# A batch of eight two-layer experts: smaller pieces for the last two w2, and x cast and transposed inside a first layer

## The chip, the cores and the metric

The kernel runs on one core of one Trainium2 chip. The metric is the device time of one execution in microseconds. A profile is one further execution, of which the hardware profiler recorded every instruction and every DMA packet.

In the profile the engines are PE (TensorE, matmuls), PEld (its weight loads, which overlap the matmuls), DVE (VectorE), ACT (ScalarE), POOL (GpSimd) and SP (SyncE). L83 is line 83 of the kernel before.

## The reference

```python
n_experts, capacity, hidden, expert_hidden = 8, 256, 512, 2048
x:  (8, 256, 512)    w1: (8, 512, 2048)    w2: (8, 2048, 512)    all float32

h = np.matmul(x, w1)
h = np.maximum(h, 0)
return np.matmul(h, w2).astype(np.float32)
```

For each of eight experts, 256 rows of 512 go through a first layer to 2048 values with a ReLU, and through a second layer back to 512. Each w1 and each w2 is 4 MB of float32, so 67 MB of weights are read once and used once.

## The kernel before, in words

Weights are cast from float32 to bfloat16 by the DMA that loads them, on POOL's queue (`load_w1`, L57, and `load_w2`, L63). x is loaded as float32 on SP's queue (`load_x`, L53) and cast to bfloat16 by ACT (L67). Results are written as float32 on SP's queue (L121), the last half of the last one on ACT's (L119).

**One expert.** `transpose_x(e)` casts x (L67), transposes it in eight 128x128 blocks on TensorE through an identity (L71) into one PSUM tile `pt_tr`, and copies that to SBUF as `xt_sb` on DVE (L75). `first_layer(e)` makes the hidden values transposed, in eight groups `g` of two blocks of 128 hidden values. Each group is eight matmuls (L83: two blocks, four steps over the 512 inputs) into a PSUM tile `pt_h`, and one ReLU into `ht_sb`: on ACT for even groups (L93), on DVE for odd ones (L91). `second_layer(e)` runs 16 steps `kt` over the hidden values (called row groups of w2 here), each with two matmuls (L107), one for each half `mt` of the 256 rows, into the PSUM tiles `po[0]` and `po[1]`. DVE copies the first to `out_sb` (L115), ACT the second (L116).

**How rows are dealt.** Weights and x are viewed so that each partition holds consecutive rows of its matrix in memory: partition p of w2 has rows 16p to 16p+15. A slice `lo:hi` of row groups is therefore one contiguous run for each partition.

**The order of the work.** The kernel's engines run in the order in which the code issues: it is a manual schedule, and the framework adds only the semaphore waits. The order of the layers is

```python
    for e in range(E - 3):
        order += [(1, e), (2, e)]
    order += [(1, e) for e in range(E - 3, E)] + [(2, e) for e in range(E - 3, E)]
```

so experts 0 to 4 run layer by layer, and then come the first layers of experts 5, 6 and 7 and after them their second layers. All weight loads are issued ahead in the same order, each held back only by its buffer: there are four buffers for w1 and four for w2. At most eight loads are in flight on POOL's queue; each later one waits until the one eight issues before it has landed. The x of four experts is loaded at the start, and that of expert e + 4 after the second layer of expert e.

Before the change `transpose_x(e + 1)` is called after `first_layer(e)`. On ACT the cast stands behind the ReLUs of that first layer; on TensorE the transposes stand between the first layer and what follows, and wait for the cast.

The w2 of the last expert comes in four pieces of 6, 5, 3 and 2 row groups; every other weight comes in one DMA. In the last second layer the last four matmuls are put in order of `mt`, so that `po[0]` is finished two matmuls ahead of `po[1]`. Its output is written in two halves.

**Buffers that matter.** PSUM: four tiles `ps_h` (for `pt_h`) and four `ps_o` (for `pt_tr` and `po` in turn). SBUF: two each of `x_bf` and `xt_sb`, four of `ht_sb`, three of `out_sb`, four of `x_sb`.

Of the kernel before, what the change touches and what calls it, by code (L numbers as in the profile page):

```python
# [1 line left out]

# [5 lines left out]


@with_exitstack  # L10
def kernel(
    ctx: ExitStack,
    tc: tile.TileContext,
    x: bass.AP,
    w1: bass.AP,
    w2: bass.AP,
    out: bass.AP,
):
    nc = tc.nc
    P = 128  # L20
    bf = mybir.dt.bfloat16
    f32 = mybir.dt.float32

    E, C, H = x.shape
    F = w1.shape[2]
    MT = C // P
    KT1 = H // P
    KT2 = F // P
    AHEAD = 4


    x_r = x.rearrange("e (p mt) k -> e p mt k", p=P)
    w1_r = w1.rearrange("e (p kt) n -> e p kt n", p=P)
    w2_r = w2.rearrange("e (p kt) n -> e p kt n", p=P)
    out_r = out.rearrange("e (p mt) n -> e p mt n", p=P)

    const = ctx.enter_context(tc.tile_pool(name="const", bufs=1))
    wpool = ctx.enter_context(tc.tile_pool(name="weights", bufs=4))
    xpool = ctx.enter_context(tc.tile_pool(name="xs", bufs=AHEAD))
    tpool = ctx.enter_context(tc.tile_pool(name="xts", bufs=2))  # L40
    hpool = ctx.enter_context(tc.tile_pool(name="hidden", bufs=4))
    opool = ctx.enter_context(tc.tile_pool(name="outs", bufs=3))
    ps_h = ctx.enter_context(tc.tile_pool(name="ps_h", bufs=4, space=bass.MemoryType.PSUM))
    ps_o = ctx.enter_context(tc.tile_pool(name="ps_o", bufs=4, space=bass.MemoryType.PSUM))

    x_sb, w1_sb, w2_sb, xt, ht = {}, {}, {}, {}, {}


    ctx.enter_context(tc.manual_schedule())

    def load_x(e):
        x_sb[e] = xpool.tile([P, MT, H], f32, tag="x", name="x_sb")
        nc.sync.dma_start(x_sb[e][:], x_r[e])  # L53

    def load_w1(e):
        w1_sb[e] = wpool.tile([P, KT1, F], bf, tag="w1", name="w1_sb")
        nc.gpsimd.dma_start(w1_sb[e][:], w1_r[e])  # L57

    def load_w2(e):
        w2_sb[e] = wpool.tile([P, KT2, H], bf, tag="w2", name="w2_sb")  # L60
        cuts = (0, KT2) if e < E - 1 else (0, 6, 11, 14, 16)
        for lo, hi in zip(cuts, cuts[1:]):
            nc.gpsimd.dma_start(w2_sb[e][:, lo:hi, :], w2_r[e, :, lo:hi, :])  # L63

    def transpose_x(e):
        x_bf = tpool.tile([P, MT, H], bf, tag="xb", name="x_bf")
        nc.scalar.copy(x_bf[:], x_sb[e][:])  # L67
        pt = ps_o.tile([P, KT1, MT, P], bf, tag="ps_o", name="pt_tr")
        for kt in range(KT1):
            for mt in range(MT):  # L70
                nc.tensor.transpose(  # L71
                    pt[:, kt, mt, :], x_bf[:, mt, kt::KT1], identity[:]
                )
        xt[e] = tpool.tile([P, KT1, C], bf, tag="xt", name="xt_sb")
        nc.vector.tensor_copy(xt[e][:], pt[:].rearrange("p k m q -> p k (m q)"))  # L75

    def first_layer(e):
        ht[e] = hpool.tile([P, KT2, C], bf, tag="ht", name="ht_sb")
        for g in range(KT2 // 2):
            ph = ps_h.tile([P, 2, C], f32, tag="ps_h", name="pt_h")  # L80
            for i in range(2):
                for kt in range(KT1):
                    nc.tensor.matmul(  # L83
                        ph[:, i, :],
                        w1_sb[e][:, kt, 2 * g + i::KT2],
                        xt[e][:, kt, :],
                        start=(kt == 0),
                        stop=(kt == KT1 - 1),
                    )
            if g % 2:  # L90
                nc.vector.tensor_relu(ht[e][:, 2 * g:2 * g + 2, :], ph[:])  # L91
            else:
                nc.scalar.activation(  # L93
                    ht[e][:, 2 * g:2 * g + 2, :], ph[:],
                    mybir.ActivationFunctionType.Relu,
                )

    def second_layer(e):
        last = e == E - 1
        po = [  # L100
            ps_o.tile([P, H], f32, tag="ps_o", name=f"pt_o{mt}") for mt in range(MT)
        ]
        order = [(kt, mt) for kt in range(KT2) for mt in range(MT)]
        if last:
            order = order[:-4] + [(kt, mt) for mt in range(MT) for kt in (KT2 - 2, KT2 - 1)]
        for kt, mt in order:
            nc.tensor.matmul(  # L107
                po[mt][:],
                ht[e][:, kt, mt * P:(mt + 1) * P],
                w2_sb[e][:, kt, :],  # L110
                start=(kt == 0),
                stop=(kt == KT2 - 1),
            )
        o = opool.tile([P, MT, H], f32, tag="o", name="out_sb")
        nc.vector.tensor_copy(o[:, 0, :], po[0][:])  # L115
        nc.scalar.copy(o[:, 1, :], po[1][:])  # L116
        if last:
            nc.sync.dma_start(out_r[e, :, 0, :], o[:, 0, :])
            nc.scalar.dma_start(out_r[e, :, 1, :], o[:, 1, :])  # L119
        else:  # L120
            nc.sync.dma_start(out_r[e], o[:])  # L121


    order = []
# [4 lines that stand above are left out]
    for e in range(AHEAD):  # L129
        load_x(e)  # L130
    for layer, e in order:
        (load_w1 if layer == 1 else load_w2)(e)
        if (layer, e) == (1, 0):
            identity = const.tile([P, P], bf, name="identity")
            make_identity(nc, identity)
    transpose_x(0)
    for layer, e in order:
        if layer == 1:
            first_layer(e)
            if e + 1 < E:  # L140
                transpose_x(e + 1)
        else:
            second_layer(e)
            if e + AHEAD < E:
                load_x(e + AHEAD)


# [1 line left out]
_INS = ['x', 'w1', 'w2']  # L149
_OUTS = [((8, 256, 512), 'float32')]  # L150


# [23 lines left out]
```

## Time and profile before

| | |
|---|---|
| device time, median of 9 runs | 188.21 us (186.73 to 188.51) |
| the profiled execution: its own time | 188.45 us |
| the profiled execution: span from first to last instruction | 186.7 us (186.67) |
| TensorE matmuls, busy | 131.1 us, 70% of the span |
| ACT, DVE, POOL busy | 32.7, 33.2 and 10.9 us |
| mean granted TensorE clock | 0.936 |
| moved by DMA | 42.06 MB (bytes written), 225 GB/s in the mean |
| weights on POOL's queue | 33.56 MB, 84.6% of 16 engines' span |
| x and outputs on SP's queue | 8.13 MB, 11.6% |
| waits of first layers for w1 (L83) | 29.9 us in 8 waits |
| waits of second layers for w2 (L107) | 10.1 us in 6 waits |
| waits of transposes for the cast (L71) | 10.6 us in 8 waits |
| cast of one x on ACT | 1038 ns |

The span leaves out 1.78 us of the execution's own time. In the page each digit of a row is the busy share of one fortieth of the span, in tenths. Lines of an order of time give the start and the length in microseconds, then engine, line, operation, output and input, and in brackets the idle time of the engine before it and what ended it. Lines that run on without idle time are put together, with a count.

### The profile page before, as it was taken

Reading aid. Unit: us, or ns where it says so; the run is one execution under the profiler, and the core shown is the slowest. Engines: PE = TensorE matmul, PEld = TensorE weight load, DVE = VectorE, ACT = ScalarE, POOL = GpSimd, SP = SyncE. Lnnn points to the kernel's source line nnn. Section 1 sums busy time; section 2 is a strip of 40 time slices with the busy share of each in tenths; the row PEclk is TensorE's granted clock in tenths of the full one; section 3 lists DMA queues with packets and bytes.
Section 4 is the critical chain, followed back from the end, with each engine's and each line's share of the span. In section 5 each row is a group of like instructions: output and inputs, shape, how many; then the busy total and the mean of one; then the engine's idle time right before and its main releaser. Section 6 shows DMA issues by size and latency. Waiting matters only on the chain.

```text
span 186.7 us, 1887 instructions
## 1 busy us (share of the span) xinstructions
PE 131.1 (70%) x825; PEld 90.2 (48%) x832; DVE 33.2 (18%) x48; ACT 32.7 (17%) x49; POOL 10.9 (6%) x25
## 2 busy tenths in 40 slices
PE   0203969488494988749895696929879693959990
PEld 0103954187141884337741594408778691414440
DVE  0100240114101141101411032011433331010101
ACT  3100330124001150102401123012514230010101
POOL 7300010101000000000111101001000000000000
PEclk9999999999879699965999789996999999988999
DMA  6999999999999999999999999999999999999913
GB/s 218 269 215 239 249 215 225 225 236 240 213 274 216 251 231 224 255 219 257 240 218 266 209 262 234 222 266 209 252 231 225 221 225 207 193 215 263 214 58 114
DMA packets 5193, 42.06 MB, mean 225 GB/s; under 512 B 577, under 2 KB 577, under 8 KB 3265
## 3 DMA queue, kind: packets, MB, share of 16 engines
q0 software_dynamic: 2736, 33.56, 84.6%
q1 hardware_dynamic: 2304, 8.13, 11.6%
q10 hardware_dynamic: 144, 0.26, 0.4%
q8 instruction: 6, 0.10, 0.2%
q14 instruction: 3, 0.02, 0.0%
HBM read 71.30 MB, written 4.19 MB: 404 GB/s over the span
## 4 chain that ended last, share of the span: by engine, by line
PE 54%; DMA 25%; another core or an unknown queue 12%; ACT 3%; issue 2%; POOL 1%; DVE 0%; ACTq 0%; POOLq 0%
PE pt_o L107 28%; PE pt_h L83 25%; DMA w_sb<-in_w_dram 25%; ACT x_bf L67 3%; PE pt_tr L71 2%; POOL w_sb L57 1%; DVE out_sb L115 0%; POOL w_sb L63 0%; POOL identity masks.py:199 0%; POOL identity masks.py:197 0%; ACT ht_sb L93 0%; ACTq L116 0%; POOLq masks.py:199 0%; ACTq L93 0%
## 5 line engine op out<-in xcount | busy, mean ns | idle before, releaser
L83 PE MATMUL pt_h<-xt_sb,w_sb 128*128 128x256 bf16 x512 | 66.4, 297 | 29.9 <-DMA w_sb<-in_w_dram 29.9
L83 PEld LDWEIGHTS <-w_sb 128*128 128x128 bf16 x512 | 60.5, 148 | 36.9 <-DMA w_sb<-in_w_dram 33.0
L107 PE MATMUL pt_o<-w_sb,ht_sb 128*128 128x512 bf16 x249 | 59.4, 395 | 10.5 <-DMA w_sb<-in_w_dram 10.1
L107 PEld LDWEIGHTS <-ht_sb 128*128 128x128 bf16 x256 | 25.8, 101 | 42.3 <-issue 15.6
L91 DVE TENSOR_SCALAR ht_sb<-pt_h 128x512 bf16<-128x512 f32 x32 | 22.1, 692 | 75.1 <-PE pt_h L83 75.1
L93 ACT ACTIVATE ht_sb<-pt_h 128x512 bf16<-128x512 f32 x32 | 19.1, 597 | 74.6 <-PE pt_h L83 74.6
L116 ACT COPY out_sb<-pt_o 128x512 f32<-128x512 f32 x8 | 4.7, 586 | 72.5 <-PE pt_o L107 72.5
L115 DVE COPY out_sb<-pt_o 128x512 f32<-128x512 f32 x8 | 5.5, 692 | 63.2 <-PE pt_o L107 63.2
L71 PE MATMUL pt_tr<-identity,x_bf 128*128 128x128 bf16 x64 | 5.5, 233 | 10.6 <-ACT x_bf L67 10.6
L71 PEld LDWEIGHTS <-x_bf 128*128 128x128 bf16 x64 | 4.1, 119 | 12.2 <-ACT x_bf L67 12.2
L57 POOL DMA_DIRECT2D w_sb<-in_w_dram x8 | 4.4, 556 | 75.9 <-PE pt_h L83 75.1
L67 ACT CAST x_bf<-x_sb 128x1024 bf16<-128x1024 f32 x8 | 8.3, 1038 | 2.2 <-DMA x_sb<-in_x_dram 2.2
L63 POOL DMA_DIRECT2D w_sb<-in_w_dram x11 | 6.0, 543 | 39.8 <-DMA w_sb<-in_w_dram 24.1
L75 DVE COPY xt_sb<-pt_tr 128x1024 bf16<-128x1024 bf16 x8 | 5.5, 692 | 11.3 <-PE pt_tr L71 11.3
L67 ACT ACT_TABLE_LOAD x1 | 1.3, 1283 | 0.7 <-PEq L160 0.7
masks.py:199 POOL TENSOR_SCALAR_AFFINE_SELECT identity<-identity 128x128 bf16<-128x128 bf16 x1 | 0.3, 288 | 0.1
masks.py:197 POOL MEMSET identity<- 128x128 bf16 x1 | 0.2, 223 | 0.0
L160 POOL MEMSET const-float32-0.0<- 128x1 f32 x1 | 0.1, 100 | 0.2 <-issue 0.2
L160 POOL MEMSET const-uint8-127<- 128x1 uint8 x1 | 0.1, 103 | 0.0
L160 POOL MEMSET const-bfloat16-1.0<- 128x1 bf16 x1 | 0.1, 102 | 0.0
L160 POOL MEMSET const-float32-1.0<- 128x1 f32 x1 | 0.1, 100 | 0.0
## 6 DMA issues: line engine op xcount, KB each, us to landing
w_sb<-in_w_dram POOLq DMA_DIRECT2D x15, 2048.0 KB, 66.6
x_sb<-in_x_dram SPq DMA_DIRECT2D x8, 512.0 KB, 25.6
out_dram<-out_sb SPq DMA_DIRECT2D x7, 512.0 KB, 15.0
w_sb<-in_w_dram POOLq DMA_DIRECT2D x1, 768.0 KB, 70.0
w_sb<-in_w_dram POOLq DMA_DIRECT2D x1, 640.0 KB, 70.0
w_sb<-in_w_dram POOLq DMA_DIRECT2D x1, 384.0 KB, 60.6
w_sb<-in_w_dram POOLq DMA_DIRECT2D x1, 256.0 KB, 51.1
out_dram<-out_sb ACTq DMA_DIRECT2D x1, 256.0 KB, 2.6
```

What stands on the lines that cost most here:

```text
L57: nc.gpsimd.dma_start(w1_sb[e][:], w1_r[e])
L63: nc.gpsimd.dma_start(w2_sb[e][:, lo:hi, :], w2_r[e, :, lo:hi, :])
L67: nc.scalar.copy(x_bf[:], x_sb[e][:])
L71: nc.tensor.transpose(pt[:, kt, mt, :], x_bf[:, mt, kt::KT1], identity[:])
L75: nc.vector.tensor_copy(xt[e][:], pt[:].rearrange("p k m q -> p k (m q)"))
L83: nc.tensor.matmul(ph[:, i, :], w1_sb[e][:, kt, 2 * g + i::KT2], xt[e][:, kt, :], start=(kt == 0), stop=(kt == KT1 - 1),)
L91: nc.vector.tensor_relu(ht[e][:, 2 * g:2 * g + 2, :], ph[:])
L93: nc.scalar.activation(ht[e][:, 2 * g:2 * g + 2, :], ph[:], mybir.ActivationFunctionType.Relu,)
L107: nc.tensor.matmul(po[mt][:], ht[e][:, kt, mt * P:(mt + 1) * P], w2_sb[e][:, kt, :], start=(kt == 0), stop=(kt == KT2 - 1),)
L115: nc.vector.tensor_copy(o[:, 0, :], po[0][:])
L116: nc.scalar.copy(o[:, 1, :], po[1][:])
L160: nc = _bacc.Bacc("TRN2", target_bir_lowering=False, num_devices=1)
```

## The change

It has three parts.

1. w2 of expert 6 comes in three DMAs (6, 5 and 5 row groups) instead of one, and w2 of expert 7 in seven (4, 4, 3, 2, 1, 1 and 1) instead of four.
2. The last second layer runs its matmuls in the same plain order as the others.
3. The cast and the transposes part company. `first_layer(e)` starts with the cast of x of the next expert, and halfway, before its fifth group, it issues the transposes of that x and the copy to `xt_sb`. Nothing is transposed after a first layer any more.

```diff
     def load_w2(e):
         w2_sb[e] = wpool.tile([P, KT2, H], bf, tag="w2", name="w2_sb")
-        cuts = (0, KT2) if e < E - 1 else (0, 6, 11, 14, 16)
+        cuts = {E - 2: (0, 6, 11, 16), E - 1: (0, 4, 8, 11, 13, 14, 15, 16)}.get(e, (0, KT2))
         for lo, hi in zip(cuts, cuts[1:]):
             nc.gpsimd.dma_start(w2_sb[e][:, lo:hi, :], w2_r[e, :, lo:hi, :])
 
+    def cast_x(e):
+        xb[e] = tpool.tile([P, MT, H], bf, tag="xb", name="x_bf")
+        nc.scalar.copy(xb[e][:], x_sb[e][:])
+
     def transpose_x(e):
-        x_bf = tpool.tile([P, MT, H], bf, tag="xb", name="x_bf")
-        nc.scalar.copy(x_bf[:], x_sb[e][:])
         pt = ps_o.tile([P, KT1, MT, P], bf, tag="ps_o", name="pt_tr")
         for kt in range(KT1):
             for mt in range(MT):
                 nc.tensor.transpose(
-                    pt[:, kt, mt, :], x_bf[:, mt, kt::KT1], identity[:]
+                    pt[:, kt, mt, :], xb[e][:, mt, kt::KT1], identity[:]
                 )
...
     def first_layer(e):
+        if e + 1 < E:
+            cast_x(e + 1)
         ht[e] = hpool.tile([P, KT2, C], bf, tag="ht", name="ht_sb")
         for g in range(KT2 // 2):
+            if g == KT2 // 4 and e + 1 < E:
+                transpose_x(e + 1)
             ph = ps_h.tile([P, 2, C], f32, tag="ps_h", name="pt_h")
...
         order = [(kt, mt) for kt in range(KT2) for mt in range(MT)]
-        if last:
-            order = order[:-4] + [(kt, mt) for mt in range(MT) for kt in (KT2 - 2, KT2 - 1)]
         for kt, mt in order:
...
+    cast_x(0)
     transpose_x(0)
     for layer, e in order:
         if layer == 1:
             first_layer(e)
-            if e + 1 < E:
-                transpose_x(e + 1)
         else:
             second_layer(e)
```

More of the change, by code (lines that the diff above doesn't have):

```diff
@@ L44 @@
     ps_o = ctx.enter_context(tc.tile_pool(name="ps_o", bufs=4, space=bass.MemoryType.PSUM))
-    x_sb, w1_sb, w2_sb, xt, ht = {}, {}, {}, {}, {}
+    x_sb, xb, xt, w1_sb, w2_sb, ht = {}, {}, {}, {}, {}, {}
     ctx.enter_context(tc.manual_schedule())
```

## The prediction

> **What bounds the kernel now.** I read the page first (slices and queues), then the order of time of TensorE, then a table of stretches at the end, then the issues of the weights. Part 2 and 3 of the page:
>
> ```profile
> PEclk9999999999879699965999789996999999988999
> DMA  6999999999999999999999999999999999999913
> ...
> q0 software_dynamic: 2736, 33.56, 84.6%
> ```
>
> The DMA engines are full in every slice but the first and the last two, and POOL's queue, which carries only weights, has 84.6% of all 16 engines' time. TensorE is idle 30% of the span. So up to about 177 us the kernel runs at the pace of the weight stream, and what TensorE saves there it waits for in the next layer. The end is different. TensorE's order of time, and the last copies:
>
> ```profile
> 135.38 0.64 PE L71 MATMUL pt_tr<-identity,x_bf 128*128 128x128 bf16 x8 [0.75 <-ACT x_bf L67]
> 137.19 7.21 PE L83 MATMUL pt_h<-xt_sb,w_sb 128*128 128x256 bf16 x64 [1.18 <-DMA w_sb<-in_w_dram]
> 145.15 0.64 PE L71 MATMUL pt_tr<-identity,x_bf 128*128 128x128 bf16 x8 [0.75 <-ACT x_bf L67]
> 146.99 7.21 PE L83 MATMUL pt_h<-xt_sb,w_sb 128*128 128x256 bf16 x64 [1.20 <-DMA w_sb<-in_w_dram]
> 157.08 7.07 PE L107 MATMUL pt_o<-w_sb,ht_sb 128*128 128x512 bf16 x31 [2.88 <-DMA w_sb<-in_w_dram]
> 166.40 15.65 PE L107 MATMUL pt_o<-w_sb,ht_sb 128*128 128x512 bf16 x63 [2.26 <-DMA w_sb<-in_w_dram]
> ...
> 175.02 0.69 DVE L115 COPY out_sb<-pt_o 128x512 f32<-128x512 f32 x1 [10.37 <-PE pt_o L107]
> 175.18 0.59 ACT L116 COPY out_sb<-pt_o 128x512 f32<-128x512 f32 x1 [10.42 <-PE pt_o L107]
> 182.13 0.59 ACT L116 COPY out_sb<-pt_o 128x512 f32<-128x512 f32 x1 [6.37 <-PE pt_o L107]
> 182.14 0.69 DVE L115 COPY out_sb<-pt_o 128x512 f32<-128x512 f32 x1 [6.42 <-PE pt_o L107]
> ```
>
> The reader should see that every layer before 166 starts on a DMA wait, and that from 166.40 the second layers of experts 6 and 7 run as one block of 63 recorded matmuls without a wait. Stretches of that end (us, busy time and count of PE, PEld, DVE, ACT, POOL, then clock, DMA share, GB/s):
>
> ```profile
> 157.03:164.14 7.11, 7.01 (x31) 3.13 (x32) 0.17 (x1) 0.00 (x0) 0.00 (x0) 1.00 1.04 221
> 164.14:166.40 2.26, 0.00 (x1) 0.00 (x0) 0.52 (x1) 0.59 (x1) 0.00 (x0) 1.00 0.87 179
> 166.40:175.20 8.80, 8.74 (x32) 3.60 (x33) 0.18 (x1) 0.02 (x1) 0.00 (x0) 0.81 1.04 238
> 175.20:177.50 2.30, 2.30 (x12) 1.08 (x11) 0.52 (x1) 0.57 (x1) 0.00 (x0) 1.00 0.88 241
> 177.50:182.10 4.60, 4.55 (x22) 1.86 (x19) 0.00 (x0) 0.00 (x0) 0.00 (x0) 1.00 0.11 44
> ```
>
> TensorE idles 2.26 us for the whole of w2 of expert 6, then runs at a mean clock of 0.81 (0.50 for about 3.4 us), and from 177.5 on the DMA engines have almost nothing left while TensorE still has 4.6 us to do. The weights are all there at 177.5, as the issues tell:
>
> ```profile
> 126.37 0.53 POOL L63 DMA_DIRECT2D w_sb<-in_w_dram  x1 [10.20 <-DMA w_sb<-in_w_dram]
> ```
>
> ```profile
> w_sb<-in_w_dram POOLq DMA_DIRECT2D x1, 256.0 KB, 51.1
> ```
>
> 126.37 + 51.1 = 177.5: the last piece (two row groups) waits 4 us for TensorE. So the bound changes hands at 166: weights before, TensorE after, with 2.26 us lost to idling and about 1.7 us to the half clock (3.4 us at half speed).
>
> **What the Trainium skill says.** "TensorE: Matmul & The Clock Gate", Part 1 (the HAM clock gate): a free-running window of about 3.4 us halves the clock after too idle a window. The trace agrees in size (0.50 for 3.4 us from 166.3), and shows it for a window that was about 37% busy; one 46% busy before 156 stayed at full clock. "DMA: Bandwidth & Descriptors", Queues, rings and completion order: each engine takes turns between queues, packet by packet. The trace agrees: the output of expert 5, issued at 164.8 behind the weights, takes until 173.2 to land, that of expert 6, issued when the weights are nearly through, 3.0 us. The same page, Anatomy of one DMA: about 2.0 us fixed per DMA from GpSimd, mostly the write receipt. Here it does not add up along the queue: the three-row piece issued at 115.65 lands 60.6 later at 176.3, the two-row piece at 177.5, 1.2 us apart.
>
> **The change, part by part.**
>
> *w2 of expert 6 in three pieces (6, 5, 5 row groups).* w2 of 5 lands at 157.03, of 6 at 166.36: 0.583 us a row group, so the pieces land near 160.5, 163.5 and 166.4. Its second layer can follow that of expert 5 at 164.14 at once. Two pieces are there, the third is needed 22 matmuls of 0.213 us later, at 168.8. At 32 x 0.213 = 6.8 us it ends at 171.0 rather than 175.0. The idling and the half clock both go; what is late next is w2 of expert 7.
>
> *w2 of expert 7 in seven pieces (4, 4, 3, 2, 1, 1, 1).* Total bytes are the same. I count time per DMA engine (eight packets each per piece) from the packet records: packets of 16,384, 6,144, 5,120, 3,072 and 2,048 bytes written take 1.227, 0.474, 0.398, 0.248 and 0.173 us; consecutive starts are some 0.02 closer (0.154 at 2,048), so time is nearly in proportion to bytes. A one-row packet of 1,024 bytes is not shown. Bounds: half of the 2,048 one, 0.086, and all of it, 0.173. I take the lower end, since the final output's 2,048-byte packets need only 0.086 and proportion holds down to 2,048. With semaphore packets (0.02 each) five more pieces then cost some 0.2 us; at the upper end 24 x 0.087 = 2.1 us.
>
> *The output of expert 6 moves.* With TensorE done at 171.0 it is issued at 171.8 instead of 175.8. Then its eight packets per engine of 0.165 us, 1.3 us, go in between those of w2 of 7. Before, its first packet went at 176.63, when the slowest engine was 0.5 us from its end. So w2 of 7 is delayed by about 1.1 us (bounds 0 and 1.3). Last piece: 177.5 + 1.1 + 0.2 = 178.8.
>
> *Last matmuls.* TensorE starts expert 7 at 171.0. The first four row groups landed near 169.3, eight near 172.5, eleven near 174.5, then 176.4, 177.3, 178.1, 178.8; a row group costs it 0.43. It keeps up and waits for each late piece. End: 178.8 + 0.05 + 2 x 0.213 = 179.3 instead of 182.07: 2.8 us.
>
> *The plain order of the last two row groups* puts the end of po0 one matmul before po1, not two. Before, the two-matmul lead gave nothing: both copies started at 182.13. In expert 5 with the plain order the copies start 0.2 apart (163.97, 164.18), so this may give 0.1. The output then follows as before: 182.14 to 186.67 is 4.5 us.
>
> *Cast and transposition inside the first layer.* Eight casts of 1.04 us (ACT), 64 transposes (0.64 us per expert on TensorE) and eight copies of 0.69 us (DVE) stay, moved. TensorE no longer waits 0.75 us seven times plus a few tenths for the last relu. Some 1.6 us leave the gap between layers, 0.64 of it entering the first layer. What hides this is the wait for weights that follows (1.18, 1.20, 2.88 us above; 3.7 before experts 4 and 5): I price it at nothing; without that cover it would be worth 7 x 1.0 = 7 us or so. ACT's cast now stands ahead of the four relus, which free pt_h for TensorE. It waits for x, last for expert 7: issued at 101.4, at most 27.4 later (128.8), needed before the relu at 138.3. Expert 1 needs it by 18.8 and x of it is among the first loads. DVE has the copy between relus; with 0.69 in each 1.75 us it has room. The release of w1 to POOL comes up to 0.64 later; weights lie 66.6 us (median) in the queue, so none runs dry. SP's outputs and x loads move up to 1.6 us earlier, same bytes.
>
> *POOL's issues.* Five more of 0.53 us. Each waits for the piece eight issues before it; the last for the second piece of expert 6, about 163.5, some 15 us before it is due. Nothing else of use is queued behind.
>
> *Sum.* 186.7 - 2.8 - 0.1 = 183.8 of span. The profiled execution's own time is 188.45 with a span of 186.67, 1.78 outside. 183.8 + 1.78 = **185.6**. The nine times lie in two groups, near 186.8 and near 188.4, 1.7 apart, the cost of one half-clock window; the median of 188.21 stands in the upper group with the profiled one, 0.24 below it. The changed end is set by the stream and shouldn't split so.
>
> **The rivals.**
> - *Half clock in the last layer.* TensorE now waits for pieces, so a window could fall below the busy share. For it: the 37% case. Against: from 174.5 on it has 2.6 us of work in each 3.4 at first, then 2.1 in 3.5, above 46%. Price from 0.43 (the last pair alone) to 1.7: 186.0 to 187.3, say 186.5.
> - *A floor under small packets.* Upper bound above, 2.1 us: 187.7, no change. Against: proportion in five sizes.
> - *The pieces change nothing at TensorE*, if the second layer of 6 still waits for its whole tile: 188.4, or 186.8 in the other group. Against: each group of matmuls in the new program waits on its own piece's semaphore.
> - *Slower: completions in series.* If each one-row piece takes the skill's 2.0 us after the one ahead, instead of 0.7, the last three add 3.9: landing at 182.7, 189.5. It decides in POOL's queue, from a last landing of 181.6 on (no gain), and 182.5 for slower by 0.5%. Against: 1.2 us between the last two pieces above; for: no one-row piece is shown.
>
> **How the numbers follow.** Forecast 0.66 (own range 184.9 to 186.6), half clock 0.14, floor 0.07, nothing changed 0.06, completions 0.07. Half a per cent, 0.94 us, is about what a measurement here can tell: faster is below 187.27, slower above 189.15. Faster: 0.66 + 0.12 + 0.02 + 0.02 = 0.82; slower 0.06 of the completions; the rest, 0.12, the same. From 184.7 to 187.7 leaves out the completions, the unchanged case, the upper part of the floor and 0.03 below.
>
> **What would show it.** Second layer of 6 starting near 164.2 with no wait and full clock; expert 7's starting near 171 and then waiting on DMA, the longest wait about a microsecond; the last piece landing near 178.8; last copies near 179.4; output of 6 issued near 171.8; DMA share full to 178. Wrong if the one-row pieces land over 1 us apart, if a clock of 0.5 appears after 171, or if waits before 157 grow.

## The result, and the profile after

The changed kernel takes 185.8 us (median of 18 runs, 185.6 to 186.23). The kernel before took 186.9 us in the runs beside it (median of 55, 186.66 to 189.0). The ratio is 0.992 (95% interval 0.990 to 0.994). It compares all executions: those of the kernel before lie in two groups, 37 near 186.8 and 18 near 188.4, and the second group draws the ratio below that of the two medians, 0.994. One execution of the kernel before, of 270 us, is left out of everything below. The profiled execution has a span of 183.9 us instead of 186.7, and its own time is 185.71 instead of 188.45; the one before was of the slower group.

The page's slices and POOL's queue, after:

```profile
PEclk9999999969999998897999669997899969999999
DMA  5999999989999999999999999999999998999973
...
q0 software_dynamic: 3456, 33.56, 86.4%
```

In the DMA row the second slice from the end holds 7 tenths instead of 1: the stream and the work now end almost together. The clock's dips now all lie before 151 us; the one near the end is gone.

The order of time of TensorE, and the last copies:

```profile
146.91 8.82 PE L89 MATMUL pt_h<-xt_sb,w_sb 128*128 128x256 bf16 x64 [2.26 <-DMA w_sb<-in_w_dram]
156.59 15.70 PE L111 MATMUL pt_o<-w_sb,ht_sb 128*128 128x512 bf16 x70 [0.86 <-DMA w_sb<-in_w_dram]
172.60 3.30 PE L111 MATMUL pt_o<-w_sb,ht_sb 128*128 128x512 bf16 x14 [0.31 <-DMA w_sb<-in_w_dram]
176.58 2.98 PE L111 MATMUL pt_o<-w_sb,ht_sb 128*128 128x512 bf16 x10 [0.68 <-DMA w_sb<-in_w_dram]
...
170.44 0.69 DVE L119 COPY out_sb<-pt_o 128x512 f32<-128x512 f32 x1 [6.27 <-PE pt_o L111]
170.60 0.59 ACT L120 COPY out_sb<-pt_o 128x512 f32<-128x512 f32 x1 [6.32 <-PE pt_o L111]
179.64 0.59 ACT L120 COPY out_sb<-pt_o 128x512 f32<-128x512 f32 x1 [8.46 <-PE pt_o L111]
179.85 0.69 DVE L119 COPY out_sb<-pt_o 128x512 f32<-128x512 f32 x1 [8.72 <-PE pt_o L111]
```

From 156.59 the second layers of 5 and 6 and the start of 7 run as one block; the wait of 2.26 us ahead of expert 6 is gone. The copies of expert 6 start at 170.4 instead of 175.0. TensorE's waits now lie inside expert 7, and are short. Stretches of the end (us, busy time and count of PE, PEld, DVE, ACT, POOL, then clock, DMA share, GB/s):

```profile
163.65:170.60 6.95, 6.90 (x33) 3.14 (x32) 0.68 (x2) 0.59 (x1) 0.43 (x1) 1.00 1.04 239
170.60:172.60 2.00, 1.69 (x8) 0.69 (x7) 0.53 (x1) 0.59 (x1) 0.00 (x0) 1.00 1.08 236
172.60:177.50 4.90, 4.22 (x18) 1.74 (x18) 0.00 (x0) 0.00 (x0) 0.00 (x0) 1.00 1.09 251
177.50:179.60 2.10, 1.88 (x7) 0.48 (x5) 0.00 (x0) 0.00 (x0) 0.00 (x0) 1.00 0.22 35
```

The clock is whole throughout, and the DMA engines are full until about 177.5, 2 us before TensorE is done. In those 2 us they move little: some of the 16 engines are still at the last pieces while the others have finished. The chain that ended last, in order of time (start, length, what), closes like this:

```profile
163.56 15.37 DMA w_sb<-in_w_dram
178.93 0.04 issue
178.97 0.61 PE pt_o L111 x2
179.58 0.27 issue
179.85 0.69 DVE out_sb L119
```

The last piece lands at 178.93 and two matmuls follow. (Landing times here and below are those of the last of a transfer's 16 semaphore increments in the trace.) Before, TensorE had 4.6 us of work left when the last piece landed (177.47 to 182.07).

### The profile page after: what moved, and what is told of

It is laid out like the page before. It is cut to its first block, busy times and chain, and to the rows that moved or that the text cites. A ratio compares the mean times of both kernels' runs of the same rounds, so it can differ in the third digit from the quotient of the medians.

```text
span 183.9 us, 1894 instructions
## 1 busy us (share of the span) xinstructions
PE 131.2 (71%) x825; PEld 90.9 (49%) x832; DVE 32.5 (18%) x48; ACT 32.8 (18%) x49; POOL 13.5 (7%) x30
## 4 chain that ended last, share of the span: by engine, by line
another core or an unknown queue 38%; DMA 33%; PE 18%; POOL 4%; issue 3%; DVE 0%; POOLq 0%
DMA w_sb<-in_w_dram 33%; PE pt_o L111 9%; PE pt_h L89 9%; POOL w_sb L63 3%; POOL w_sb L57 1%; PE pt_tr L73 0%; DVE out_sb L119 0%; POOL identity masks.py:199 0%; POOL identity masks.py:197 0%; POOLq masks.py:199 0%; POOLq L174 0%; POOLq L63 0%; POOLq L163 0%
## 5 line engine op out<-in xcount | busy, mean ns | idle before, releaser
L89 PE MATMUL pt_h<-xt_sb,w_sb 128*128 128x256 bf16 x512 | 69.7, 303 | 31.2 <-DMA w_sb<-in_w_dram 31.2
L89 PEld LDWEIGHTS <-w_sb 128*128 128x128 bf16 x512 | 61.7, 149 | 39.3 <-DMA w_sb<-in_w_dram 34.4
L111 PE MATMUL pt_o<-w_sb,ht_sb 128*128 128x512 bf16 x249 | 58.4, 387 | 11.9 <-DMA w_sb<-in_w_dram 11.4
L63 POOL DMA_DIRECT2D w_sb<-in_w_dram x16 | 8.6, 540 | 74.0 <-DMA w_sb<-in_w_dram 66.1
L57 POOL DMA_DIRECT2D w_sb<-in_w_dram x8 | 4.4, 556 | 76.2 <-PE pt_h L89 75.4
L73 PEld LDWEIGHTS <-x_bf 128*128 128x128 bf16 x64 | 4.7, 116 | 5.2 <-ACT x_bf L67 5.2
```

What stands on the lines that cost most here:

```text
L73: nc.tensor.transpose(pt[:, kt, mt, :], xb[e][:, mt, kt::KT1], identity[:])
L89: nc.tensor.matmul(ph[:, i, :], w1_sb[e][:, kt, 2 * g + i::KT2], xt[e][:, kt, :], start=(kt == 0), stop=(kt == KT1 - 1),)
L111: nc.tensor.matmul(po[mt][:], ht[e][:, kt, mt * P:(mt + 1) * P], w2_sb[e][:, kt, :], start=(kt == 0), stop=(kt == KT2 - 1),)
```

## The experiments

Each is told as a change of the kernel before or of the changed kernel. Ratios are to the kernel before in the runs beside it, over all executions as above.

**The pieces alone** (of the kernel before):

```diff
-        cuts = (0, KT2) if e < E - 1 else (0, 6, 11, 14, 16)
+        cuts = {E - 2: (0, 6, 11, 16), E - 1: (0, 4, 8, 11, 13, 14, 15, 16)}.get(e, (0, KT2))
```

> The pieces alone: both new lists of cuts, with cast, transposes and the order of the last matmuls as before. Theory (the whole gain comes from the pieces, the moves are hidden by the wait for weights): as the changed kernel, 185.8 us, ratio about 0.993, span near 184, last piece landing near 178.9. Rival (the moves carry a part): at most half of the gain is left, 186.4 or more against 186.9 of the kernel before.

Measured: 186.24 us, ratio 0.994 (0.992 to 0.996), span 184.2, last landing 178.76. That lies between the theory and the rival: the early start of expert 6 and the late last landing are there, but 0.4 us against the changed kernel is missing. Something else in the change carries that, the moves or the plain order.

**The moves alone**: the changed kernel with the old cuts and the old order of the last four matmuls.

```diff
-        cuts = {E - 2: (0, 6, 11, 16), E - 1: (0, 4, 8, 11, 13, 14, 15, 16)}.get(e, (0, KT2))
+        cuts = (0, KT2) if e < E - 1 else (0, 6, 11, 14, 16)
...
         order = [(kt, mt) for kt in range(KT2) for mt in range(MT)]
+        if last:
+            order = order[:-4] + [(kt, mt) for mt in range(MT) for kt in (KT2 - 2, KT2 - 1)]
```

> The moves alone: cast and transposes inside the first layer, old cuts and old order of the last matmuls. Theory: no change, ratio 1.00 within 0.004, since each first and second layer still starts when its weights land (w2 of 5 at 156.5 to 157, w2 of 6 at 166.4). Rival: 0.5 us or more faster.

Measured: 186.81 us, ratio 0.997 (0.994 to 1.000). TensorE's order of time at the end:

```profile
157.77 7.99 PE L113 MATMUL pt_o<-w_sb,ht_sb 128*128 128x512 bf16 x30 [0.22 <-issue]
166.45 13.97 PE L113 MATMUL pt_o<-w_sb,ht_sb 128*128 128x512 bf16 x63 [0.68 <-DMA w_sb<-in_w_dram]
```

Expert 6 starts at 166.45, as before: the moves don't shift the end. The faster groups agree too (medians 186.80 and 186.77); that only 3 of 20 executions lie above 187.7 here, and 28 of 71 of the kernel before, may be chance. This profile also shows the last block of 63 matmuls at full clock (the half-clock window fell into expert 5, 157.1 to 160.5): 13.97 us instead of 15.65 in the profile of the kernel before. Its time, 186.87, is that of the lower group of the kernel before.

**w2 of 6 in pieces, w2 of 7 as before** (of the changed kernel):

```diff
-        cuts = {E - 2: (0, 6, 11, 16), E - 1: (0, 4, 8, 11, 13, 14, 15, 16)}.get(e, (0, KT2))
+        cuts = {E - 2: (0, 6, 11, 16), E - 1: (0, 6, 11, 14, 16)}.get(e, (0, KT2))
```

> The changed kernel, but w2 of expert 7 in its four old pieces (6, 5, 3, 2). Theory: the second layer of 6 still follows that of 5 at once, the end is set by a last piece of two row groups, with four matmuls after it instead of two: 0.4 us later than the changed kernel, 186.2 us, span near 184.3, last landing near 178.7. Rival (the pieces of one row group carry the gain): 186.7 or more.

Measured: 186.12 us, ratio 0.993 (0.991 to 0.995). Without the seven pieces of expert 7, 0.8 of the 1.1 us are still there; the seven add 0.3 us. (This run has the plain order too, so the 0.8 us isn't the worth of expert 6's pieces alone.) The profile fell on an execution of 187.26 us with the clock halved from 156.4 to 163.2:

```profile
158.07 23.00 PE L111 MATMUL pt_o<-w_sb,ht_sb 128*128 128x512 bf16 x93 [0.22 <-issue]
```

TensorE then doesn't wait again and sets the end itself, at 181.1, though the last piece landed at 177.59 (not at the expected 178.7, since the output of 6 was issued later too, at 174.8, and hardly delayed it): an execution with two half-clock windows in expert 5 is bound by TensorE even with the early start.

**w2 of 7 in pieces, w2 of 6 whole** (of the changed kernel):

```diff
-        cuts = {E - 2: (0, 6, 11, 16), E - 1: (0, 4, 8, 11, 13, 14, 15, 16)}.get(e, (0, KT2))
+        cuts = {E - 1: (0, 4, 8, 11, 13, 14, 15, 16)}.get(e, (0, KT2))
```

> The changed kernel, but w2 of expert 6 in one piece. Theory: its second layer starts at 166.4 as before and TensorE sets the end, so the seven pieces of 7 gain nothing: span 186.7 with a half-clock window in the second layer of 6, 185.0 without, ratio about 1.00. Rival (the pieces of 7 carry the gain): span near 184, ratio 0.993.

Measured: 186.61 us, ratio 0.998 (0.995 to 1.001). In the order of time:

```profile
156.51 7.07 PE L111 MATMUL pt_o<-w_sb,ht_sb 128*128 128x512 bf16 x31 [0.81 <-DMA w_sb<-in_w_dram]
166.26 15.66 PE L111 MATMUL pt_o<-w_sb,ht_sb 128*128 128x512 bf16 x63 [2.68 <-DMA w_sb<-in_w_dram]
```

A wait like that of the kernel before (2.68 us, there 2.26) and the same block of 63. The last piece lands at 177.51, as before, and TensorE is done at 181.9. So the small last pieces gain nothing while expert 6 starts late; they need its early start. Against the changed kernel 0.8 us is lost. The faster group has a median of 186.5, 0.26 below that of the kernel before: no matmul waits for a late piece here, so the gain lies elsewhere. The next run traces it to the plain order.

**The old order of the last four matmuls** (in the changed kernel), to find what the pieces alone lacked:

```diff
         order = [(kt, mt) for kt in range(KT2) for mt in range(MT)]
+        if last:
+            order = order[:-4] + [(kt, mt) for mt in range(MT) for kt in (KT2 - 2, KT2 - 1)]
```

> The changed kernel, with only the old order of the last four matmuls put back. With a last piece of one row group the old order leaves three matmuls after its landing, the plain order two. Theory A (this is most of what the pieces alone lacked): one matmul of 0.21 us and little more, 186.0 to 186.25 us. Theory B (the moves of cast and transposes make the difference): as the changed kernel, 185.8 us.

Measured: 186.28 us, ratio 0.994 (0.991 to 0.996). That is the time of the pieces alone (186.24), so the moves add nothing and the plain order is worth 0.45 to 0.5 us. The end of its order of time, where the last piece landed at 179.01:

```profile
179.06 0.81 PE L113 MATMUL pt_o<-w_sb,ht_sb 128*128 128x512 bf16 x3 [0.27 <-DMA w_sb<-in_w_dram]
...
179.94 0.59 ACT L122 COPY out_sb<-pt_o 128x512 f32<-128x512 f32 x1 [8.67 <-PE pt_o L113]
179.95 0.69 DVE L121 COPY out_sb<-pt_o 128x512 f32<-128x512 f32 x1 [8.73 <-PE pt_o L113]
```

Three matmuls follow the landing instead of two: the old order keeps the matmul (14, second half) back behind (15, first half), which needs the last piece. The last matmul ends 0.85 after the landing instead of 0.63, so that is 0.2 us.

The rest comes after the last matmul. From its end to the end of the span it takes 4.64 us here and 4.34 in the changed kernel. With the old order both copies start together and the two halves of the output are issued 0.11 us apart; with the plain order DVE's copy starts 0.21 behind ACT's, and the halves are issued 0.31 apart. (Why DVE's copy starts later there is open.) ACT's half then lands 2.78 after the last matmul instead of 3.33, SyncE's half at much the same distance as before (3.45, 3.50). At the end SyncE waits for one transfer's semaphore after another, for ACT's half first, then for six others, and last for its own half. Its long waits there (us in total, times, longest), with the plain order and with the old one:

```profile
SPq L174 <- DMA out_dram<-out_sb: 1.6, 2, 1.4
SPq L176 <- DMA out_dram<-out_sb: 2.1, 1, 2.1
```

With the plain order it goes through the six others, some 0.06 us each, between the two landings and is free 0.05 us after the last. With the old order the halves land 0.17 apart, and it goes through them after both: it is free 0.31 us after the last. The other profiles agree: from the last matmul to the end of the span the kernel before and the pieces alone take 4.61 and 4.60 us, the runs with expert 6 whole and with the old pieces of 7, which have the plain order, 4.38 and 4.40.

**The output of 6 behind the weights** (in the changed kernel):

```diff
+        elif e == E - 2:
+            nc.gpsimd.dma_start(out_r[e], o[:])
         else:
             nc.sync.dma_start(out_r[e], o[:])
```

> The changed kernel, but the output of expert 6 is issued on POOL's queue, so that its packets stand behind all of w2 of 7 and don't take turns with them. Theory (the early output delays w2 of 7 by 1.1 us): the last piece lands near 177.8 instead of 178.9, and the output of 6 fills the DMA engines between then and 180; span near 182.8, 184.7 us. Rival (the delay comes from the number of small pieces, or from the engines' own spread): last landing unchanged, 178.5 or later, time 185.6 or more. If GpSimd's output DMA is slow to land, it could end last instead, above 184 in span.

Measured: 184.58 us, ratio 0.988 (0.986 to 0.989). In the profile the last piece of w2 of 7 lands at 177.68 instead of 178.93, and the output of 6 at 178.96. The early output's turns cost the weights 1.25 us, and the time falls by 1.2. The profile itself caught an execution of 185.77, with the clock halved from 156.9 to 160.3:

```profile
157.94 21.61 PE L111 MATMUL pt_o<-w_sb,ht_sb 128*128 128x512 bf16 x93 [0.22 <-issue]
```

**The output of 5 as well:**

```diff
-        elif e == E - 2:
+        elif e >= E - 3:
             nc.gpsimd.dma_start(out_r[e], o[:])
```

> As the one before, and the output of expert 5 on POOL's queue too. Theory: another 1.3 us of packets leaves the stream, the last piece would land near 176.5; TensorE, which starts expert 7 near 170.5 with 6.8 us of work, now nearly sets the end (177.4): span 182.2 to 182.6, since 2.6 us of outputs then also meet the last output. Rival: no better than with the output of 6 alone.

Measured: 184.48 us (183.81 to 185.93), ratio 0.989 (0.985 to 0.993). No better in the median, as the rival had it. The reason is TensorE:

```profile
157.48 20.88 PE L111 MATMUL pt_o<-w_sb,ht_sb 128*128 128x512 bf16 x94 [0.81 <-DMA w_sb<-in_w_dram]
```

The last piece lands at 177.19, but TensorE works from 157.48 to the end without a wait and is done at 178.4. The landing is later than the expected 176.5 because one DMA engine lags: fifteen of the sixteen report the last piece by 176.30.

**w2 of 5 in pieces too** (in the kernel just told):

```diff
-        cuts = {E - 2: (0, 6, 11, 16), E - 1: (0, 4, 8, 11, 13, 14, 15, 16)}.get(e, (0, KT2))
+        cuts = {E - 3: (0, 6, 11, 16), E - 2: (0, 6, 11, 16),
+                E - 1: (0, 4, 8, 11, 13, 14, 15, 16)}.get(e, (0, KT2))
```

> The outputs of 5 and 6 behind the weights, and w2 of expert 5 in three pieces too (6, 5, 5). Theory (with the outputs out of the way TensorE's late start of expert 5 at 157 sets the end): the second layer of 5 starts near 154.5, TensorE is ahead of the pieces again, the end follows the last landing near 176.5 to 177.2: about 183.7 us, with less spread. Rival (the stream sets the end already): no better than 184.5.

Measured: 183.44 us (183.23 to 183.49), ratio 0.979 (0.975 to 0.982). Its order of time:

```profile
154.08 11.82 PE L111 MATMUL pt_o<-w_sb,ht_sb 128*128 128x512 bf16 x52
166.64 4.31 PE L111 MATMUL pt_o<-w_sb,ht_sb 128*128 128x512 bf16 x18 [0.74 <-DMA w_sb<-in_w_dram]
171.52 5.71 PE L111 MATMUL pt_o<-w_sb,ht_sb 128*128 128x512 bf16 x24 [0.56 <-DMA w_sb<-in_w_dram]
177.31 0.59 ACT L120 COPY out_sb<-pt_o 128x512 f32<-128x512 f32 x1 [7.73 <-PE pt_o L111]
```

TensorE is 2.5 us ahead and waits for pieces again; the end follows the last landing (176.59). This version beats both kernels: 2.4 us less than the changed one. That TensorE's late start held the run before it back is shown by this.

**Sixteen pieces of one row group for w2 of 7** (in the changed kernel):

```diff
-        cuts = {E - 2: (0, 6, 11, 16), E - 1: (0, 4, 8, 11, 13, 14, 15, 16)}.get(e, (0, KT2))
+        cuts = {E - 2: (0, 6, 11, 16), E - 1: tuple(range(KT2 + 1))}.get(e, (0, KT2))
```

> The changed kernel, but w2 of expert 7 in sixteen pieces of one row group. Theory (time of a packet in proportion to its bytes, completions not in series): nine more pieces cost 0.1 to 0.5 us in the last landing, time 185.8 to 186.3. Rival 1 (a floor of 0.173 us under small packets): ruled out for three pieces by the packet records, would give 128 x 0.087 = 6 us or more. Rival 2 (completions in series, 2 us each): over 195 us.

Measured: 186.62 us, ratio 0.998 (0.995 to 1.000). Both rivals fall, but the cost is above the theory's: 0.8 us for nine more pieces. The last piece lands at 179.42, 0.5 later than with seven pieces, and the end follows it as in the changed kernel (in this profile the clock was halved from 156.8 to 160.2, and TensorE was still just early enough):

```profile
179.47 0.59 PE L111 MATMUL pt_o<-w_sb,ht_sb 128*128 128x512 bf16 x2 [0.40 <-DMA w_sb<-in_w_dram]
```

The remaining 0.3 us lies outside this profile's span (2.2 us outside instead of 1.8); why is open.

**Without the weights, before and after.** Both kernels load w1 and w2 of expert 0 alone and use them for every expert, so this leaves 59 MB of reads out and computes something else.

```diff
     def load_w1(e):
+        if e:
+            w1_sb[e] = w1_sb[0]
+            return
```

and the same in `load_w2`.

> The kernel before with w1 and w2 loaded for expert 0 alone; the other experts use these, so that no layer after the first waits for weights. Theory: TensorE sets the time; seven gaps of about 1.6 us stand between a first layer and what follows it, while TensorE waits for the last ReLU and the cast and then transposes. Time about 16.8 (first weights) + 8 x 14 + 7 x 1.6 and the tail, some 150 us. To be compared with the next run.

> The changed kernel with the same loads left out. Theory (moving cast and transposes is worth about 1.0 us per expert once nothing hides it): 6 to 8 us less than the run before it. Rival (the moves are worth nothing even then, since the transposes only change place): within 2 us of it.

Measured: 148.39 and 140.73 us, one execution each: 7.7 us less. The order of time around one transposition, of the kernel before:

```profile
72.94 0.64 PE L77 MATMUL pt_tr<-identity,x_bf 128*128 128x128 bf16 x8 [0.75 <-ACT x_bf L73]
73.62 6.85 PE L113 MATMUL pt_o<-w_sb,ht_sb 128*128 128x512 bf16 x31
```

and of the changed kernel:

```profile
66.53 0.61 PE L79 MATMUL pt_tr<-identity,x_bf 128*128 128x128 bf16 x8
66.98 3.67 PE L95 MATMUL pt_h<-xt_sb,w_sb 128*128 128x256 bf16 x32
```

The wait for the cast is gone. The moves save TensorE about 1.1 us per expert in the mean, seven times: 0.93 where a second layer follows (one expert takes 15.28 us before and 14.35 after), and more where another first layer follows, which before waited 0.78 us for `xt_sb` too. Almost none of it is the plain order: from the last matmul to the end of the span the two differ by 0.04 us. The stream of weights hides all of it in the real kernel.

**TensorE's gap filled** (in the kernel before, nothing but unread matmuls added):

```diff
         else:
+            if e == E - 2:
+                spare = ps_h.tile([P, H], f32, tag="ps_h", name="pt_spare")
+                for i in range(9):
+                    nc.tensor.matmul(spare[:], ht[e - 1][:, i, :P], w2_sb[e - 1][:, i, :], start=True, stop=True)
             second_layer(e)
```

> The kernel before with nine matmuls that nothing reads (1.9 us at full clock) in TensorE's idle time between the second layers of 5 and 6; the result stays the same. Theory (the times near 188.4 are those in which the second layer of 6 falls into a half-clock window, after a window with too little work): nearly all times near 186.75, none or few near 188.4; no 0.50 clock in the second layer of 6. Rival (the two groups come from something else, such as the DMA): both groups stay as frequent, about a third near 188.4.

Measured: 186.79 us, ratio 0.997 (0.995 to 1.000); 6 of 20 times lie above 187.7, where 17 of 37 of the kernel before do. The two counts could differ by chance, but not where the times lie: the 17 are all between 188.25 and 188.57, and of these 20 none is; five lie between 187.76 and 188.10, one at 189.22. So the group near 188.4 is gone when the gap before expert 6 is filled, as the theory had it, and a smaller slow group has come in its place. The profiled one took 189.22. Its clock was halved from 156.1 to 163.0, in expert 5, so that the added matmuls came too late and pushed expert 6:

```profile
166.82 2.11 PE L146 MATMUL pt_spare<-w_sb,ht_sb 128*128 128x512 bf16 x9
168.76 13.98 PE L107 MATMUL pt_o<-w_sb,ht_sb 128*128 128x512 bf16 x62
```

So the idle time ahead of expert 5 was followed by half clock here, and filling one gap does not stop that. In the kernel before such a delay is hidden by the wait for w2 of 6 (the run of the moves alone shows it: half clock in expert 5, and 186.87 us); here the added matmuls take that room. That the five times near 188 are of this kind too is not shown, since none of them was profiled.

## Why the prediction was right, point by point

*The bound at the end.* It was TensorE's late start on expert 6. Leave out the three pieces of 6, and 0.8 of the 1.1 us are lost, the pieces of 7 giving nothing; leave out the seven of 7, and 0.3 are lost.

*w2 of 6 in three pieces.* Predicted at 164.2 and done at 171.0; measured 163.65 and about 170.6. The difference is that of w2 of 5, which landed at 156.55 instead of 157.03.

*w2 of 7, and the output that moves.* The seven landings were predicted near 169.3, 172.5, 174.5, 176.4, 177.3, 178.1 and 178.8, and came at 169.32, 172.56, 174.41, 176.54, 177.63, 178.28 and 178.93. The 1.1 us for the early output was measured by itself as 1.25. The one-row packets took 0.098 us, nearer to the lower bound (0.086) than to the upper (0.173). This rules out the floor, and 0.65 us between the last landings rules out completions in series.

*The plain order* was mis-sized. It was priced at 0.1 us, from the starts of the two copies; leaving it out costs 0.45 to 0.5. The step looked at when po0 ends and overlooked that the old order holds one more matmul behind the last piece (0.2 us); the sum counted two matmuls, which is the plain order's number, so this part was in the total under another name. And "the output then follows as before" was not so: from the last matmul to the end of the span it took 4.34 us instead of 4.61, through the order in which the two halves are issued and land. The first copy didn't start earlier: in this last layer DVE's copy starts 0.21 after ACT's, though its tile is finished first.

*The moves* cost and gave nothing: with the old order put back the time is that of the pieces alone. Without the cover of the weights they are worth 7.7 us, predicted some 7.

*Half clock in the last layer.* It did not come in the profile, and no run of the changed kernel exceeds 186.23. But the same window earlier, in expert 5, makes TensorE the bound in executions of its variants (187.26 with two windows, 185.77 with one, above). The prediction priced that case inside the last layer only.

*The sum.* 2.9 us of span predicted, 2.8 measured; 185.6 predicted, 185.8 measured. Some of this closeness is luck: the last matmul ended at 179.6 instead of 179.3 (the landing 0.13 late, and the last matmul takes 0.38 us to its end, not the 0.21 from one start to the next), and the output after it was 0.27 us shorter instead of 0.1. The median that the forecast stood beside, 188.21, came from nine runs of which five lay in the upper group; over 55 runs it is 186.9. The gain against that is 1.1 us, not 2.6: in executions without the half-clock window in expert 6, the window's 1.7 us was not there to be removed. That this window makes the upper group fits the profiles (188.45 with it in the kernel before, 188.07 with it in the run with expert 6 whole, 186.87 without it in the run of the moves alone), and the group near 188.4 went when the gap was filled.

*Two readings.* The last landing at which the change would have been slower by 0.5% comes out at 178.8 + (189.15 - 185.6) = 182.35, not 182.5. And on the boundaries of the recorded clock TensorE was busy for some 34% of the window before 166.4 and 42% of that before 156.2, not 37% and 46%; that a window 46% busy keeps the full clock is not a rule here, as the last section shows.

## What to carry to other kernels

Where a stream of transfers is the bound, look at what is left after its last byte, and at every engine's backlog at that time: small last pieces pay only when the consumer is already waiting. Look for outputs that share the DMA engines with the last inputs: here one of 512 KB delayed the end by 1.25 us, about its own transfer time, and behind the last input it filled time in which the engines had nothing else to do. Before pricing a reordering at next to nothing, count what stands behind the last arrival in each order, and look at when each part of the last output is issued.

## What the runs showed of the hardware that was not expected

- Packets of 1,024 bytes, cast on the way, took 0.098 us and those of 2,048 bytes 0.173. Three pieces of 128 KB (written) landed 0.65 us apart on one queue, so here the completion of one did not hold up the next. With sixteen such pieces the last landed 0.5 us later than with seven.
- The 16 DMA engines do not finish a piece together: in the profile of the changed kernel ten reported the last piece between 177.55 and 177.95, and the other six between 178.65 and 178.93. The slowest one sets the landing.
- When the clock halves. In the twelve profiles with all weights the profile's record of the granted clock consists of stretches of full and of half clock, whose lengths are multiples of about 3.42 us. Cut into windows of that length, and with the share of each in which a matmul is on record as running: all 72 windows at full clock that were busy for 41.5% or less were followed by half clock, all above 46.2% by full clock, and between these two shares both occurred. At half clock the border lies elsewhere: the 19 windows busy for 77% or less were followed by half clock again, the 74 from 80% on by full clock. (The ends of matmuls are modelled, and some are missing from the record, so the shares are rough.)
- So what an idle gap does depends on where it falls among these windows. In the kernel before, the 2.88 us ahead of 157.08 were shared by two windows, the first 42% busy, and the clock stayed full; in the run of the moves alone, the 2.75 us ahead of 157.01 lay in one window, 20% busy, and the clock was halved. In this way, as far as the profiles and the filled gap show, executions of one and the same kernel come to differ by 1.7 us, half of such a window.
